# Layer 1 begun with eight units by quarters of K, and layer 0's first block cut in halves

## The chip, the cores and the metric

The kernel runs on one core of one Trainium2 chip. The metric is the device time of one execution in microseconds, the median of several runs. The engines of the core are TensorE (PE: matmuls; PEld: its weight loads), VectorE (DVE), ScalarE (ACT), GpSimd (POOL) and SyncE (SP), which issues nearly all loads here; 16 DMA engines move the data.

## The reference

A trunk of two layers on a residual stream x of 256 tokens by 2048 channels, all in float32:

```python
cond = silu(c)
for i in range(2):
    shift, scale, gate = split(cond @ ada_w[i] + ada_b[i], 3)     # ada_w[i]: 2048 x 6144
    h = rmsnorm(x, norm_w[i]) * (1 + scale) + shift
    out = ssd_mixer(h, ...) if i == 0 else mlstm_mixer(h, ...)
    x = x + gate * out
return rmsnorm(x, final_norm_w)
```

The first mixer (a state-space mixer, SSD) projects h to z (4096), x (4096), B and C (1024 each) and dt (64); x, B and C go through a causal convolution of 4 taps and a SiLU. Eight groups are mixed over the tokens, multiplied by SiLU(z), normalized per group and projected back (4096 to 2048). The second (mLSTM, 8 heads) projects h to q and k (4096 together, convolved likewise), v, o and z (4096 each) and 16 gates, mixes per head, normalizes, multiplies by SiLU(z) and projects back.

## The kernel before

**Tiles.** Channels lie on partitions, so x^T and h^T are 16 chunks (K chunks) of 128 x 256. A *unit* is a block of 512 output columns of one projection: 4 weight tiles of 128 x 2048 (a quarter of K each, 1 MB of 2^20 bytes), each loaded in two halves of 128 x 1024 into `raw` (6 buffers of 512 KB). ScalarE rounds a half to `hi`, VectorE subtracts to get `lo` (4 buffers each), and three matmuls (`hi` with the rounded h, `hi` with its rest, `lo` with the rounded h; lines 253 to 255) stand in for one of full precision. A half makes 24 matmuls of 128 x 256, a tile 48, a unit 192. Units of v keep tokens on partitions (lines 264 to 266: half as many matmuls of twice the width).

**Modulation products.** cond @ ada_w is made on VectorE: an *item* is two K chunks of 1024 columns (two loads of 512 KB), and for each chunk one operation adds `raw * cond[k]` to an accumulator `aacc` (line 77, 128 x 1024). After 8 items the accumulator is summed over partitions: 8 transposes on TensorE (line 202), each followed by an accumulating copy on ScalarE. A layer has 6 such column chunks, `cc` 0 to 3 for shift and scale of four K chunks of h each, 4 and 5 for the gate of the residual.

**Order.** The program is one list of items: weight tiles (`w`), modulation items (`a`), and steps that make chunks of h (`h`; each chunk two VectorE operations, `htmp` and `hT`, and one on ScalarE). It is written out by constants: `PRE`, `START`, `ADA_AT`, `POST`, `K1`, `DEF1`. Loads are issued on SP in the list's order, 3 items ahead; splits are issued 3 halves ahead of their matmuls. What follows a unit (convolutions, SSD, mLSTM) are Python generators that are stepped once per half (`run_bg`), so that their operations come between splits and matmuls.

**Layer 0** begins with the 9 units of `PRE`, taken by blocks of K: `START` = 4, 4, 4, 4 chunks. In each block every unit gets one weight tile. The first two units keep their two PSUM banks (pool `pj`, 4 banks) through all blocks; the other 7 use two banks of pool `pm` (4 banks, tile `ms`) for a block and are then *parked*: ScalarE copies the first block's banks to SBUF, VectorE adds those of later blocks (`park`). `ada_items(0, cc)` for the next block come between the weight tiles at the places `ADA_AT`. Then `POST` follows: further units, and three passes of the output projection (`op`), over groups 0 to 2, 3 and 4, 5 to 7. Its tuples (q, n) put n modulation items of queue q among that entry's tiles; queue 0 holds `cc` 4 and 5 of layer 0, queue 1 the chunks 0 to 3 of layer 1, but for the last `DEF1`.

**Layer 1** begins, after the row statistics (`to_layer1`: 12 chunks of h at once), with the units o and z of head 0 by quarters of K, the one late modulation item among them. Then come the gates' tile, and head by head qk, v, o and z, each unit whole. The gates' chain (`gates_done`: softplus, two scans, transposes) must be through before any head's mixing (`gen_ml`). Output passes stand after head 3 and at the end.

The lines that drive this at the beginning of layer 0 and of layer 1:

```python
cuts = grid(START)
items.extend(sh_sc(*cuts[0]))
for i, (k, n) in enumerate(cuts):
    items.append(dict(kind="h", layer=0, ks=range(k, k + n)))
```

## Time and profile before

| | |
|---|---|
| Median of 3 runs | 1799.52 us (1786.51 to 1804.31) |
| Profiled execution, first to last instruction (span) | 1784.4 us; no other time is recorded for it; the shortest run is 2.1 us above it |
| TensorE busy, mean granted clock | 1696.1 us (95%), 0.979 |
| VectorE busy | 1295.9 us (73%) |
| ScalarE busy | 923.6 us (52%) |
| Read from HBM | 390.41 MB; 220 GB/s with what is written, over the span |

Busy time is a union of the instructions' spans, and matmuls overlap, so a share of 95% is no measure of how much faster TensorE could go. The clock is the share of full speed that was granted, 0.5 or 1.0 at any moment; a stage's figure is the mean. Times in the trace are microseconds from the first instruction.

### The profile page before, as it was taken

What the parts mean: (1) busy time and instruction counts of PE and PEld (TensorE: products, weight loads), DVE (VectorE), ACT (ScalarE), POOL (GpSimd) and SP (SyncE); (2) the same over time, 40 slices, a digit from 0 to 9 for tenths busy, and PEclk for the clock granted to TensorE, in tenths of its full rate; (3) what the DMA queues carried; (4) which work ended last, traced back from release to release, by engine and by line L of the source; (5) the groups of instructions that cost most, each with busy time, mean ns of one, the idle gap of its engine ahead of it and who ended that gap; (6) DMA issues with size and microseconds to landing.
All of it is one profiled execution on the core that took longest, in us unless ns stands there. A gap on an engine that the chain in (4) does not pass through costs nothing.

```text
span 1784.4 us, 32951 instructions
## 1 busy us (share of the span) xinstructions
PE 1696.1 (95%) x13285; PEld 1633.0 (92%) x13285; DVE 1295.9 (73%) x1615; ACT 923.6 (52%) x1571; POOL 97.4 (5%) x127
## 2 busy tenths in 40 slices
PE   2999999999899899899999999999999999999997
PEld 2998999999899889899898989899989898989996
DVE  6789899999886789886777776646455555564554
ACT  3443557998553487445455445544345454454442
POOL 0000003222200020000000000000000000000000
PEclk6999999999999999999999999999999999999998
DMA  9988856566776885894666676545555555554551
GB/s 359 327 305 300 291 183 209 184 201 219 264 247 219 276 298 193 295 339 167 230 227 235 235 259 209 188 169 186 184 183 173 181 171 184 175 180 170 185 178 71
DMA packets 110377, 394.74 MB, mean 221 GB/s; under 512 B 14352, under 2 KB 14352, under 8 KB 110224
## 3 DMA queue, kind: packets, MB, share of 16 engines
q1 hardware_dynamic: 107856, 392.54, 64.5%
q8 instruction: 104, 1.70, 0.4%
q0 software_dynamic: 2368, 0.09, 0.1%
q14 instruction: 49, 0.40, 0.1%
HBM read 390.41 MB, written 2.10 MB: 220 GB/s over the span
## 4 chain that ended last, share of the span: by engine, by line
PE 68%; DVE 11%; issue 11%; DMA 5%; ACT 3%; POOL 1%; SPq 0%; ACTq 0%; POOLq 0%; DVEq 0%
PE pj L253 16%; PE pj L254 16%; PE pj L255 16%; DVE aacc L77 4%; DVE lo L81 4%; PE pj L264 3%; PE pj L265 3%; PE pj L266 3%; DMA raw<-in_ada 3%; PE ms L253 2%; PE ms L254 2%; PE ms L255 2%; ACT hi L73 1%; DMA raw<-in_wss 1%; PE ms L202 1%
## 5 line engine op out<-in xcount | busy, mean ns | idle before, releaser
L73 ACT ACTIVATE hi<-raw 128x1024 fp32r<-128x1024 f32 x548 | 580.9, 1062 | 719.9 <-PE pj L254 496.8
L81 DVE TENSOR_TENSOR lo<-raw,hi 128x1024 fp32r<-128x1024 f32 x548 | 670.0, 1225 | 321.9 <-ACT hi L73 318.9
L253 PE MATMUL pj<-hT,hi 128*128 128x256 f32 x2400 | 683.8, 285 | 4.3 <-ACT hT L73 4.3
L254 PE MATMUL pj<-hT,hi 128*128 128x256 f32 x2400 | 676.4, 282 | 0.5 <-DVE hT L77 0.5
L255 PE MATMUL pj<-hT,lo 128*128 128x256 f32 x2400 | 674.6, 281 | 1.3 <-DVE lo L81 1.3
L253 PEld LDWEIGHTS pj<-hT,hi 128*128 128x128 f32 x2400 | 456.7, 191 | 5.7 <-ACT hT L73 4.9
L254 PEld LDWEIGHTS pj<-hT,hi 128*128 128x128 f32 x2400 | 456.7, 190 | 1.7 <-issue 0.8
L255 PEld LDWEIGHTS pj<-hT,lo 128*128 128x128 f32 x2400 | 455.8, 190 | 2.1 <-DVE lo L81 1.7
L253 PE MATMUL pj<-y,hi 128*128 128x256 f32 x1024 | 292.2, 285 | 0.0
L254 PE MATMUL pj<-y,hi 128*128 128x256 f32 x1024 | 291.8, 285 | 0.0
L255 PE MATMUL pj<-y,lo 128*128 128x256 f32 x1024 | 291.4, 285 | 0.0
L77 DVE SCALAR_TENSOR_TENSOR aacc<-raw,cond,aacc 128x1024 f32<-128x1024 f32 x180 | 236.0, 1311 | 40.4 <-DMA raw<-in_ada 38.8
L253 PEld LDWEIGHTS pj<-y,hi 128*128 128x128 f32 x1024 | 197.2, 193 | 0.6 <-issue 0.3
L254 PEld LDWEIGHTS pj<-y,hi 128*128 128x128 f32 x1024 | 197.4, 193 | 0.0
L255 PEld LDWEIGHTS pj<-y,lo 128*128 128x128 f32 x1024 | 197.2, 193 | 0.0
L253 PE MATMUL ms<-hT,hi 128*128 128x256 f32 x448 | 127.2, 284 | 2.3 <-DVE park L81 2.0
L255 PE MATMUL ms<-hT,lo 128*128 128x256 f32 x448 | 126.2, 282 | 0.8 <-DVE lo L81 0.8
L254 PE MATMUL ms<-hT,hi 128*128 128x256 f32 x448 | 126.2, 282 | 0.0
L264 PE MATMUL pj<-hi,hT 128*128 128x512 f32 x256 | 101.8, 398 | 0.0
L265 PE MATMUL pj<-hi,hT 128*128 128x512 f32 x256 | 101.4, 396 | 0.0
L266 PE MATMUL pj<-lo,hT 128*128 128x512 f32 x256 | 101.2, 395 | 0.0
L253 PEld LDWEIGHTS ms<-hT,hi 128*128 128x128 f32 x448 | 85.2, 190 | 3.5 <-DVE park L81 2.6
(175 smaller groups left out, 1557.9 us busy)
## 6 DMA issues: line engine op xcount, KB each, us to landing
raw<-in_wml SPq DMA_DIRECT2D x256, 512.0 KB, 4.0
raw<-in_ada SPq DMA_DIRECT2D x192, 512.0 KB, 5.2
raw<-in_wss SPq DMA_DIRECT2D x160, 512.0 KB, 4.9
raw<-in_wso SPq DMA_DIRECT2D x64, 512.0 KB, 5.1
raw<-in_wmo SPq DMA_DIRECT2D x64, 512.0 KB, 3.6
xT<-in_xt SPq DMA_DIRECT2D x4, 512.0 KB, 6.2
out<-o SPq DMA_DIRECT2D x4, 512.0 KB, 4.0
raw<-in_wdt SPq DMA_DIRECT2D x2, 512.0 KB, 3.1
```

What stands on the lines that cost most here:

```text
L73: nc.scalar.activation(out, in_, func, **kw)
L77: nc.vector.scalar_tensor_tensor(out, a, s, b, op0, op1)
L81: nc.vector.tensor_tensor(out, a, b, op)
L202: nc.tensor.transpose(ps[:, sl], acc[:, c * P:(c + 1) * P], ident)
L253: nc.tensor.matmul(o, hi[:, w0:w0 + P], ah, start=first, stop=False, skip_group_check=True)
L254: nc.tensor.matmul(o, hi[:, w0:w0 + P], al, start=False, stop=False, skip_group_check=True)
L255: nc.tensor.matmul(o, lo[:, w0:w0 + P], ah, start=False, stop=last, skip_group_check=True)
L264: nc.tensor.matmul(o, ah[:, s], wh, start=(k == 0), stop=False)
L265: nc.tensor.matmul(o, al[:, s], wh, start=False, stop=False)
L266: nc.tensor.matmul(o, ah[:, s], wl, start=False, stop=(k == u.ktot - 1))
```

## The change

1. `START` becomes 2, 2, 4, 4, 4, and the first block's modulation comes as two parts (`ada_small`, now with 4 pieces of 256 columns per load, read by 1 KB rows): 4 items with products of 512 columns before the first two chunks of h, 4 more among the first half block's tiles, `cc` 1 among the second's. The half blocks use a half of each weight tile. Parked units are parked once more.
2. Layer 1 begins with 8 units by quarters of K (`K1`): o and z of head 0 in PSUM, qk, v of head 0 and qk, v, o, z of head 1 parked in SBUF (three of the four buffers `y`). `mm` learns to close a group of the v kind before parking.
3. `DEF1` = 16: 16 of the 32 items for shift and scale of layer 1 (`cc` 2 and 3) leave `POST` and stand one behind each tile of the first two quarters. `to_layer1` makes 8 chunks of h; the other two fours come at their quarters.
4. The gates' tile stands before the sixth tile of the fourth quarter (`GPOS` = 5). The convolution of qk waits for the gates, and from head 2 on until the scores of head h-2 are made; v, o and z of head h first complete head h-2 (`head_over`).

```diff
-ADA_AT = [[0, 2, 3, 3, 5, 5, 5, 7], [0, 0, 4, 5, 5, 5, 8, 8], [0, 0, 0, 1, 2, 3, 7, 8]]
+ADA_AT = [[0, 2, 4, 6], [0, 1, 2, 3, 4, 5, 6, 7], [0, 0, 2, 3, 4, 5, 6, 7], [0, 0, 1, 2, 3, 4, 6, 7]]
-START = [4, 4, 4, 4]
-K1, DEF1 = [("o", 0), ("z", 0)], 1
+START = [2, 2, 4, 4, 4]
+K1 = [("o", 0), ("z", 0), ("qk", 0), ("v", 0), ("qk", 1), ("v", 1), ("o", 1), ("z", 1)]
+RES1, DEF1, GPOS = 2, 16, 5
...
-POST = [('z', 4, (0, 1)), ('dt', 0, (0, 2)), ('z', 3, (0, 1)), ('x', 3, (0, 1)), ('x', 4, (0, 1)), ('z', 6, (0, 2)), ('z', 5, (0, 3)), ('bc', 3, (0, 4), (1, 1)), ('x', 6, (0, 1)), ('op', (0, 1, 2), (1, 2)), ('x', 5, (1, 3)), ('z', 7, (1, 3)), ('x', 7, (1, 6)), ('op', (3, 4), (1, 3)), ('op', (5, 6, 7), (1, 13))]
+POST = [('z', 4, (0, 1)), ('dt', 0, (0, 2)), ('z', 3, (0, 1)), ('x', 3, (0, 1)), ('x', 4, (0, 1)), ('z', 6, (0, 2)), ('z', 5, (0, 3)),
+        ('bc', 3, (0, 4)), ('x', 6, (0, 1)), ('op', (0, 1, 2), (1, 3)), ('x', 5, (1, 1)), ('z', 7, (1, 1)), ('x', 7, (1, 1)),
+        ('op', (3, 4), (1, 3)), ('op', (5, 6, 7), (1, 7))]
...
     def ada_small(layer, cc, part):
-        return [dict(kind="a", src=ada[layer, cc, 4 * part + q], hs=(0, 1), layer=layer, key=(cc, part), q=q, nq=4,
+        def half(q, j):
+            v = ada[layer, cc, 2 * q + j].rearrange("p (r c) -> p r c", r=4)
+            return v[:, :, 256 * part:256 * (part + 1)]
+        return [dict(kind="a", src=[half(q, j) for j in range(2)], hs=(0, 1), layer=layer, key=(cc, part), q=q, nq=4,
                      w=512) for q in range(4)]
...
+            if isinstance(it["src"], list):
+                nc.sync.dma_start(raw.rearrange("p (r c) -> p r c", r=4), it["src"][half])
+            else:
+                nc.sync.dma_start(raw, it["src"][:, 1024 * half:1024 * (half + 1)])
...
-                    nc.tensor.matmul(o, ah[:, s], wh, start=(k == 0), stop=False)
+                    nc.tensor.matmul(o, ah[:, s], wh, start=(fresh and kk == 0), stop=False)
                     nc.tensor.matmul(o, al[:, s], wh, start=False, stop=False)
-                    nc.tensor.matmul(o, ah[:, s], wl, start=False, stop=(k == u.ktot - 1))
+                    nc.tensor.matmul(o, ah[:, s], wl, start=False,
+                                     stop=(kk == u.nk - 1 and (closes or (u.park is not None and ends))))
...
+    qk_used = set()
+
+    def head_over(h):
+        if h >= 2:
+            finish([held[1, h - 2]])
 
     def qk_done(h):
         def f(banks):
-            qk_t[h] = sp.tile([P, 4, T], F32, tag="a4", name=nm("qk"))
-            qk_d[h] = spawn(gen_conv(banks, "mcw", "mcb", [2 * h, 2 * h + 1, 16 + 2 * h, 17 + 2 * h], qk_t[h]))
+            def conv():
+                yield from gate_ok(lambda: "gates" in held and held["gates"].over and (h < 2 or h - 2 in qk_used))
+                qk_t[h] = sp.tile([P, 4, T], F32, tag="a4", name=nm("qk"))
+                yield from gen_conv(banks, "mcw", "mcb", [2 * h, 2 * h + 1, 16 + 2 * h, 17 + 2 * h], qk_t[h])
+            qk_d[h] = spawn(conv())
             held[1, h] = spawn(gen_ml(h))
...
     st2 = OutStat()
-    first = [ml_unit(*tok, side=i >= 2) for i, tok in enumerate(K1)]
+    first = [ml_unit(*tok, park=None if i < RES1 else parker(1, i - RES1)) for i, tok in enumerate(K1)]
     for q in range(4):
         if 4 * q >= ready1:
+            assert len(late) <= DEF1 - 8 * (q + 1 - ready1 // 4)
             items.append(dict(kind="h", layer=1, ks=range(4 * q, 4 * q + 4)))
         new = w_items(first, 4 * q, 4)
         for j, w in enumerate(new):
+            if q == 3 and j == GPOS:
+                add_unit(Unit("fm", 1, 8, 1, h_act, gates_done), [wgt])
             items.append(w)
-            n = -(-len(late) // max(1, (len(new) - j) + (ready1 // 4 - 1 - q) * len(new))) if 4 * q < ready1 else 0
+            n = -(-len(late) // max(1, len(new) - j + (2 - q) * len(new))) if q < 3 else 0
             items.extend(late[:n])
             late = late[n:]
     assert not late
     m1 = len(items)
-    add_unit(Unit("fm", 1, 8, 1, h_act, gates_done), [wgt])
```

`v_done`, `o_done` and `zp_done` call `head_over(h)` first; `parker` takes the layer as a further key.

## Rows read from the trace of the kernel before

**Rows 1.** The page: span, and TensorE's busy time.

```profile
span 1784.4 us, 32951 instructions
PE 1696.1 (95%) x13285; PEld 1633.0 (92%) x13285; DVE 1295.9 (73%) x1615; ACT 923.6 (52%) x1571; POOL 97.4 (5%) x127
```

**Rows 2.** Stages: from:to, length; busy us (instructions) by engine; clock, DMA share, GB/s.

```profile
0.00:41.55 41.55, 9.30 (x43) 7.20 (x43) 27.35 (x38) 12.86 (x40) 2.88 (x9) 0.71 0.97 363
41.55:98.35 56.80, 55.07 (x440) 54.10 (x441) 46.43 (x51) 29.63 (x53) 0.00 (x0) 0.94 0.88 312
98.35:157.58 59.23, 54.81 (x442) 53.15 (x441) 51.81 (x59) 23.95 (x40) 0.00 (x0) 0.97 0.92 320
157.58:212.94 55.36, 54.03 (x443) 51.80 (x441) 48.86 (x56) 24.00 (x38) 0.00 (x0) 1.00 0.88 306
212.94:504.68 291.74, 276.92 (x2313) 268.42 (x2312) 275.21 (x359) 221.12 (x486) 61.27 (x75) 0.98 0.63 211
504.68:573.80 69.12, 69.12 (x579) 69.12 (x578) 48.10 (x59) 29.46 (x31) 0.00 (x0) 1.00 0.67 222
573.80:658.82 85.02, 80.43 (x667) 78.48 (x666) 70.54 (x76) 49.75 (x114) 7.71 (x10) 0.96 0.85 294
658.82:726.00 67.18, 61.15 (x501) 58.87 (x500) 59.88 (x84) 48.08 (x113) 4.45 (x3) 0.97 0.67 219
726.00:806.30 80.30, 73.60 (x599) 71.22 (x598) 67.77 (x77) 35.66 (x74) 0.69 (x1) 1.00 0.91 321
806.30:883.00 76.70, 73.19 (x605) 72.98 (x606) 56.84 (x86) 35.63 (x47) 1.20 (x2) 0.97 0.56 188
...
1318.76:1413.56 94.80, 94.80 (x709) 90.08 (x707) 55.02 (x69) 45.42 (x58) 1.97 (x3) 1.00 0.53 178
```

**Rows 3.** Timeline of VectorE at the start: start, us, instruction, count.

```profile
11.53 0.75 DVE L85 TENSOR_SCALAR aacc<-raw,cond 128x1024 f32<-128x1024 f32 x1 [7.03 <-DMA raw<-in_ada]
...
18.18 15.81 DVE L77 SCALAR_TENSOR_TENSOR aacc<-raw,cond,aacc 128x1024 f32<-128x1024 f32 x12
```

**Rows 4.** Timeline of TensorE: the first projection.

```profile
41.55 1.23 PE L253 MATMUL pj<-hT,hi 128*128 128x256 f32 x4 [3.31 <-ACT hT L73]
```

**Rows 5.** Waits from 574 to 659: us in total, times, longest.

```profile
DVE aacc L77 <- DMA raw<-in_ada: 11.6, 7, 3.0
...
PE ms L202 <- ACT ms L73: 3.9, 1, 3.9
```

**Rows 6.** Waits from 659 to 800: the broadcast of groups 5 to 7's norms.

```profile
PE ms L289 <- DVE dg L85: 4.9, 2, 3.4
```

**Rows 7.** Waits from 806 to 883: the gates' transposes.

```profile
PE ms L774 <- DVE gaterow L81: 3.5, 1, 3.5
```

**Rows 8.** VectorE's groups by shape: busy us, mean ns, idle before.

```profile
L81 DVE TENSOR_TENSOR lo<-raw,hi 128x1024 fp32r<-128x1024 f32 x548 | 670.0, 1225 | 321.9 <-ACT hi L73 318.9
L77 DVE SCALAR_TENSOR_TENSOR aacc<-raw,cond,aacc 128x1024 f32<-128x1024 f32 x180 | 236.0, 1311 | 40.4 <-DMA raw<-in_ada 38.8
...
L81 DVE TENSOR_TENSOR park<-park,ms 128x512 f32<-128x512 f32 x42 | 27.8, 681 | 0.6 <-PE ms L255 0.6
...
L77 DVE SCALAR_TENSOR_TENSOR hT<-htmp,mod,hT 128x256 fp32r<-128x256 f32 x32 | 13.9, 480 | 1.5 <-ACT hT L73 1.5
...
L77 DVE SCALAR_TENSOR_TENSOR zp<-th,pj 128x512 f32<-128x512 f32 x16 | 10.9, 680 | 0.0
```

**Rows 9.** The page's DMA part: packets by size; queues with packets, MB, share.

```profile
DMA packets 110377, 394.74 MB, mean 221 GB/s; under 512 B 14352, under 2 KB 14352, under 8 KB 110224
...
q1 hardware_dynamic: 107856, 392.54, 64.5%
...
q0 software_dynamic: 2368, 0.09, 0.1%
```

**Rows 10.** Timeline of VectorE: first and last operation of the gates' chain.

```profile
858.78 0.48 DVE L85 TENSOR_SCALAR gaterow<-pj,V 128x256 f32<-128x256 f32 x1 [0.44 <-PE pj L255]
...
881.56 0.42 DVE L81 TENSOR_TENSOR gaterow<-gaterow,G 128x256 f32<-128x256 f32 x1
```

More of the change, by code (lines that the diff above doesn't have):

```diff
@@ L214, in load @@
             raw = wp.tile([P, 1024], F32, tag="raw", name=nm("raw"), bufs=RAWB)
-            nc.sync.dma_start(raw, it["src"][:, 1024 * half:1024 * (half + 1)])
+            if isinstance(it["src"], list):
+                nc.sync.dma_start(raw.rearrange("p (r c) -> p r c", r=4), it["src"][half])
+            else:
+                nc.sync.dma_start(raw, it["src"][:, 1024 * half:1024 * (half + 1)])
             it["raw"][half] = raw
@@ L549, in f @@
                 i = PRE.index(("z", g)) - RES
-                sz_t[g] = atile[i // 2][:, 1024 * (i % 2):1024 * (i % 2 + 1)].rearrange("p (b t) -> p b t", b=4)
+                sz_t[g] = atile[0, i // 2][:, 1024 * (i % 2):1024 * (i % 2 + 1)].rearrange("p (b t) -> p b t", b=4)
             z_done[g] = spawn(gen_z(banks, sz_t[g]))
@@ L662, in trunk_kernel, with parker @@
     atile = {}
-    def parker(i):
+    def parker(layer, i):
         def f():
-            if i // 2 not in atile:
-                atile[i // 2] = wp.tile([P, 2048], F32, tag="y", name=nm("park"), bufs=4)
+            key = (layer, i // 2)
+            if key not in atile:
+                atile[key] = wp.tile([P, 2048], F32, tag="y", name=nm("park"), bufs=4)
             o = 1024 * (i % 2)
-            return [atile[i // 2][:, o + 512 * j:o + 512 * (j + 1)] for j in range(2)]
+            return [atile[key][:, o + 512 * j:o + 512 * (j + 1)] for j in range(2)]
         return f
-    pre = [ssd_unit(tok, side=i >= 2) for i, tok in enumerate(PRE[:RES])] + [ssd_unit(tok, parker(i)) for i, tok in enumerate(PRE[RES:])]
+    pre = [ssd_unit(tok, side=i >= 2) for i, tok in enumerate(PRE[:RES])] + [ssd_unit(tok, parker(0, i)) for i, tok in enumerate(PRE[RES:])]
     def grid(cut):
@@ L792, in f @@
         def f(banks):
+            head_over(h)
             v_t[h] = sp.tile([P, 2, 512], F32, tag="s4c", name=nm("v"))
@@ L799, in f @@
         def f(banks):
+            head_over(h)
             to_t[h] = sp.tile([P, 4, T], F32, tag="s4b", name=nm("to"))
@@ L806, in f @@
         def f(banks):
+            head_over(h)
             zp_t[h] = sp.tile([P, 4, T], F32, tag="s4a", name=nm("zp"))
@@ L829, in gen_ml @@
             nc.tensor.matmul(ps[:, T:384], k[:, c, P:T], q[:, c, P:T], start=(c == 0), stop=(c == 1))
+        qk_used.add(h)
         yield
@@ L885, in trunk_kernel, with ml_unit @@
     ML = {"qk": (0, "fm", qk_done), "v": (1, "tm", v_done), "o": (2, "fm", o_done), "z": (3, "fm", zp_done)}
-    def ml_unit(name, h, side=False):
+    def ml_unit(name, h, park=None):
         i, kind, done = ML[name]
-        return Unit(kind, 4, 2, 4, h_act, done(h), side=side), [wml[4 * h + i, q] for q in range(4)]
+        return Unit(kind, 4, 2, 4, h_act, done(h), park=park), [wml[4 * h + i, q] for q in range(4)]
     st2 = OutStat()
-    first = [ml_unit(*tok, side=i >= 2) for i, tok in enumerate(K1)]
+    first = [ml_unit(*tok, park=None if i < RES1 else parker(1, i - RES1)) for i, tok in enumerate(K1)]
     for q in range(4):
         if 4 * q >= ready1:
+            assert len(late) <= DEF1 - 8 * (q + 1 - ready1 // 4)
             items.append(dict(kind="h", layer=1, ks=range(4 * q, 4 * q + 4)))
```

## The prediction

> **What bounds the kernel now.** I read the page first, then a table of the span cut into stages, then the waits of the stages that lose time. The page gives 95% busy for TensorE over a span of 1784.4 us [rows 1], but that hides short stalls, so the stage table [rows 2] is read by three things: TensorE's idle time, its granted clock, and what VectorE and the DMA engines do meanwhile. The stage 504.68 to 573.80 is the clean one: 12 weight tiles (1.049 MB each, 48 matmuls each by the code) in 69.12 us, TensorE never idle. That is 5.76 us a tile, so a quarter of 8 units is 46.1 us and layer 0's block of 9 units 51.8 us. Against this the other stages stand thus [rows 2]:
> - The first 41.55 us hold no projection at all: VectorE starts its first products at 11.53 when their data lands and works through them until 33.99 [rows 3]; the first projection starts at 41.55 [rows 4].
> - The three blocks from 41.55 to 212.94 take 171.4 us for 155.5 us of tiles. Each loads 17 items (9 weights, 8 modulation), 17.8 MB; DMA moved 306 to 320 GB/s in them, and 3 x 17.8 MB in 171.4 us is 312. VectorE was busy 147.1 us, 86%. These blocks are fed at the rate of the loads, with VectorE close behind.
> - 212.94 to 504.68: VectorE busy 94%. The change leaves this work as it is.
> - 573.80 to 806.30 (units x5, z7, x7 and the last two output passes): 232.5 us with 17.3 us of TensorE idle (4.6, 6.0, 6.7). The clock shares of 0.96 and 0.97 cost another 3.4 and 2.0 us: 22.7 us in all. The first of its stages loads 24 items, 25.2 MB in 85 us, and there VectorE waits 11.6 us for modulation data and TensorE 3.9 us for the transposes behind them [rows 5]; the middle one waits for groups 5 to 7 [rows 6].
> - 806.30 to 883: 3.5 us of wait for the gates' chain [rows 7]. Afterwards layer 1 runs with TensorE full, VectorE at 58% and DMA at 178 GB/s (1318.76 to 1413.56) [rows 2].
>
> So layer 0 is short of loads and VectorE time, layer 1 has both to spare; each term asks which of the two the moved work meets.
>
> **Start of layer 0, block of 4 cut into 2 and 2.** The first modulation chunk is read in two parts, each 4 items whose products are 512 wide. Sixteen such products at 0.68 us (the row of a 512-wide operation with the same opcode; this and all VectorE durations below are in [rows 8]) are 10.9 us for 22.5 us, so the last is done near 22.5. Before, 7.6 us passed from the last product to the first projection; that leaves 30, and TensorE starts 11.5 us sooner. The first half block (9 half tiles, 25.9 us) covers its VectorE work: 9 splits (11.0), 4 small items (10.9) and 2 chunks of h (two 0.48 us operations each, 1.9). The second half block does not. VectorE owes 9 splits (11.0), 8 full items (16 x 1.311 less 0.56 for the cheaper first, 20.4), two chunks of h (1.9), and for the 7 parked units a further add into SBUF, 14 x 0.681 = 9.5 that did not exist before: 42.8 us against 25.9 of matmuls. Its loads are 12.5 items, 13.1 MB, 42 us at 313 GB/s. So it ends at 30 + 25.9 + 42.8, near 99 with no gaps and 105 at the 86% that VectorE reached in these blocks; before, the next block began at 98.35. From there blocks and limits are the old ones, so the difference is carried on. The modulation pieces now come in rows of 1 KB, and no packet between 512 B and 2 KB is in the trace [rows 9]. From the nearest rows: 107856 packets of 3.6 KB took 64.5% of 16 engines, 171 ns each; 2368 tiny ones took 0.1%, 12 ns each. If the 12 ns are all overhead, four 1 KB packets cost 36 ns more than one of 4 KB, 21% of the 23 us that chunk's 8.4 MB takes at 363 GB/s: 0 to 5 us. Without any gap and without that price VectorE could be through by 89: bounds -9 and +12. I take **+3**: VectorE as the limit, nearer to its 94% than to its 86%, and a little for the short rows.
>
> **Relief of late layer 0.** Fifteen of 28 modulation items leave 573.80 to 806.30 (by the order list 3, 3, 6, 3, 13 become 1, 1, 1, 3, 7). Each takes two loads off SP's queue and two products of 1.311 us off VectorE (39 us of 198), and two of the four transposed chunks go, with their 8 transposes and 8 accumulating copies each. Stage x5 to x7 then loads 15.7 MB, 53 us at its own 294 GB/s, under its 69 us of tiles: the load wait, the transposes stuck on ScalarE and the slow clock after them go, 7 of 8.0 us. The last pass loads 19.9 MB for 26.2, 62 us at 321 GB/s: 5 of 6.7 us, the rest being the row statistics. In the middle the wait is a chain of groups 5 to 7, which 22 us less VectorE work ahead shortens: 4 of 8. Together **-16**. The bounds are 6 (only what waits for loads) and 22.7 (all that is lost).
>
> **Layer 1's first quarters.** They hold 8 units instead of 2, and 16 late items stand one behind each tile of the first two. Each quarter then loads 16 items, both together 33.6 MB against 92.2 us of tiles. At the 313 GB/s of the blocks that is 107 us, +15; if the six raw buffers (3.1 MB) start full and end empty, 97 us, +5. At 294 it is 114, +22; at 363 nothing. VectorE owes 32 splits (39.2), 32 products (40.8), 12 park adds in the second quarter (8.2) and 8 chunks of h beyond the first four, which fall in the gap between layers (7.6): 95.8 us, 102 at 94% busy, 112 at 86%: +10 to +20. I take **+11** (0 to +22). The first quarter's 12 parks are copies on ScalarE and cost nothing: in the first block, with 14 of them, it was busy 29.6 of 56.8 us [rows 2]. Were it late, the four spare PSUM banks would stop the next parked unit. The last two quarters load 8 items each with 24 further adds, 16 us beside 39 of splits in 92: free.
>
> The Trainium skill (DMA: Bandwidth & Descriptors, Specifications) puts the limit of one core's HBM reads at about 358 GB/s. At that rate this stage's loads would take 94 us, its term would be that of VectorE alone (+4 with no gap, +10 at 94% busy) and the sum below -8 to -2. Only the first 41.55 us of the trace come to such a rate, so the sum goes by the blocks.
>
> **Gates and heads.** The gates' tile now stands before the last three tiles of the fourth quarter, 17 us of cover plus whatever of unit qk2 the order puts ahead; before, some 7 half tiles of qk0 stood there (605 matmuls in the stage, 432 of them o0, z0 and the gates [rows 2]). Their chain took from 858.78 to 881.98 [rows 10]. The wait was 3.5 us and slowed the clock after it (0.97 of 76.7 us): between -5 and +3, **-1**. Two heads then start together. A head's own VectorE work is 55.0 less 32 splits, 15.8 us [rows 2, 8]; two of them, the gates and the first of the other 16 modulation items meet near 985. The new waits (v, o and z of head h complete head h-2 first; the convolution of qk waits for the gates, and from head 2 on for the scores of head h-2) hold two of four PSUM banks, and behind them the next units' matmuls on TensorE. With 40% of VectorE free there I take **+2**, between 0 and +10.
>
> **Sum.** 3 - 16 + 11 - 1 + 2 = -1 us on the profiled span of 1784.4. What lies around the span I take as unchanged: the shortest timed run is 1786.5, 2.1 us above it, the median 1799.5. On the median it gives 1798. A per cent, 18 us, is about what a measurement of this kernel can tell from no change: its three runs lie 17.8 us apart.
>
> **Rivals.** (1) *The spare room of layer 1 is real* (faster): raw buffers ahead and VectorE at 100% make the quarters cost +4, late layer 0 gives back 20 and the earlier start keeps 7: -7 - 20 + 4 - 1 + 2 = -22, 1777. For it: VectorE's 94% in 212.94 to 504.68, and 363 GB/s in the first 41.55 us. Against it: no stage with 17 items a block held more than 320 GB/s.
> (2) *VectorE is the bound wherever splits, products and park adds meet* (slower): second half block and first two quarters run at 86% busy. Place: these two stretches; price: +9 and +20; with late layer 0 at -12 (chains of groups 5 to 7 not shortened), heads +4 and gates 0 this is +21, 1820. It decides from VectorE work over about 0.9 of the stage's matmul time. For it: 86% in the three blocks, and 42.8 us of work on 25.9. Against it: there the loads were as late.
> (3) *The change does not do what it says at the start*: TensorE begins 11 us sooner and the first phase ends no sooner. That is in my sum; so it moves no number further.
>
> **How the numbers follow.** The forecast, within 1%, gets 0.48: terms cancel because the same bytes and products leave one crowded stretch for another. Rival 1 gets 0.28 and rival 2 0.24, the ends of the bounds being about as far on both sides. The forecast's own range is 1782 to 1816; for 8 in 10 it reaches past both rivals' times, 1769 to 1825. Faster by over 1% 0.28, within 0.48, slower 0.24.
>
> **What would show it.** In the profile after: first projection near 30 us; the next full block near 101, TensorE idle and at half clock in the second half block; 573.80 to 806.30's work shorter by some 16 us with no wait of transposes for late products; the first two quarters of layer 1 near 103 us with VectorE over 90% and DMA over 300 GB/s, the last two near 92. Wrong would be quarters without idle TensorE (then rival 1), or a first phase that ends 8 us or more later together with quarters near 112 us (rival 2), or a stall at the first output pass of layer 1, which I price at nothing.

## The result, and the profile after

The changed kernel takes 1814.45 us (median of 5 runs, 1796.56 to 1821.28), the kernel before beside it 1790.25 us (5 runs, 1786.04 to 1804.31): a ratio of 1.0104, 95% interval 1.0056 to 1.0151. Run again on another chip (first experiment) it gave 1.0116 (1.0085 to 1.0147). So it is a good 1% slower, 10 to 27 us; the forecast was no change. The profiled execution took 1796.56 us, the shortest of the five, with a span of 1794.9 us against 1784.4: the rows below explain 10.5 us. The page of the changed kernel, answering to [rows 1]:

```profile
span 1794.9 us, 33052 instructions
PE 1696.9 (95%) x13285; PEld 1633.1 (91%) x13285; DVE 1324.7 (74%) x1684; ACT 929.8 (52%) x1583; POOL 97.2 (5%) x127
```

TensorE does the same work. VectorE has 28.8 us more; the 50 new park adds (92 operations for 42, 62.2 us for 27.8) are more than that. The stages, cut at the same events as [rows 2] (columns as there; the second and third lines are the two half blocks):

```profile
0.00:29.91 29.91, 7.90 (x39) 6.53 (x39) 17.09 (x37) 9.75 (x30) 2.40 (x9) 0.79 0.99 332
29.91:67.04 37.13, 29.87 (x221) 29.19 (x222) 31.25 (x40) 20.64 (x35) 0.00 (x0) 0.85 0.89 293
67.04:107.16 40.12, 30.07 (x234) 28.64 (x233) 35.06 (x44) 14.39 (x30) 0.00 (x0) 0.91 0.82 302
107.16:162.93 55.77, 52.91 (x434) 52.34 (x433) 51.70 (x61) 22.14 (x37) 0.00 (x0) 0.97 0.85 312
162.93:218.21 55.28, 52.71 (x443) 51.69 (x442) 52.22 (x59) 24.25 (x39) 0.00 (x0) 1.00 0.90 326
218.21:509.05 290.84, 276.01 (x2314) 267.75 (x2313) 272.04 (x355) 220.10 (x485) 61.47 (x75) 0.99 0.64 212
509.05:578.16 69.11, 69.11 (x579) 69.11 (x577) 48.53 (x59) 29.29 (x31) 0.00 (x0) 1.00 0.69 228
578.16:654.59 76.43, 76.43 (x659) 74.88 (x658) 53.82 (x60) 49.73 (x106) 6.63 (x9) 1.00 0.64 215
654.59:720.00 65.41, 61.99 (x504) 58.89 (x503) 54.02 (x77) 45.49 (x105) 4.36 (x4) 0.97 0.59 198
720.00:810.61 90.61, 75.62 (x589) 73.09 (x587) 60.25 (x70) 33.53 (x58) 0.69 (x1) 0.93 0.73 240
810.61:861.63 51.02, 49.16 (x344) 46.21 (x345) 37.84 (x46) 27.37 (x50) 0.00 (x0) 0.95 0.76 262
861.63:908.00 46.37, 45.83 (x337) 42.67 (x336) 44.95 (x54) 21.51 (x38) 0.00 (x0) 1.00 0.96 354
908.00:954.10 46.10, 46.10 (x348) 43.92 (x348) 31.06 (x36) 18.49 (x19) 0.00 (x0) 1.00 0.56 188
```

The next block's first eight matmuls, 1.0 us, run from 101.75 on, ahead of the last 36 of the second half block, which end at 107.16. Read against [rows 2]: the last full block of layer 0 begins at 218.21 for 212.94, 5.3 us later. The long middle and the clean stage are the same within 1 us. Units x5, z7 and x7 take 76.43 us for 85.02, TensorE without a gap: 8.6 us won. But the two output passes and the gap before layer 1 take 156.0 us (654.59 to 810.61) where they took 147.5: 8.5 us lost, with TensorE idle 15.0 us and the clock at 0.93 in the second of the two stretches. (The cuts at 720 here and at 726 in [rows 2] lie some 5 us inside the last pass, in both kernels alike.) So late layer 0, from which 16 us were to come, takes 232.45 us for 232.50. Layer 1 takes 401.2 us to its first output pass (810.61 to 1211.8) for 396.7.

**The start.** VectorE's and TensorE's timelines, answering to [rows 3] and [rows 4], and the one long stall of each half block:

```profile
11.85 0.49 DVE L88 TENSOR_SCALAR aacc<-raw,cond 128x512 f32<-128x512 f32 x1 [7.42 <-DMA raw<-in_ada]
...
18.24 7.05 DVE L80 SCALAR_TENSOR_TENSOR aacc<-raw,cond,aacc 128x512 f32<-128x512 f32 x9
...
29.91 0.58 PE L262 MATMUL pj<-hT,hi 128*128 128x256 f32 x1 [2.81 <-ACT hT L76]
...
50.69 0.66 PE L208 MATMUL ms<-ident,aacc 128*128 128x128 f32 x2 [7.14 <-DVE aacc L80]
...
92.02 0.66 PE L208 MATMUL ms<-ident,aacc 128*128 128x128 f32 x2 [8.60 <-DVE aacc L80]
```

TensorE begins 11.6 us sooner and gives it back in two waits, 15.7 us in all, each for the last product of a modulation chunk whose transposes stand at the head of its queue: 7.1 us in the first half block, with 120 of its 216 matmuls behind them, and 8.6 us in the second. Before, no such wait between 41 and 213 was longer than 1.1 us. The price of a 512-wide product was 0.75 us, not 0.68; VectorE's groups by shape, answering to [rows 8]:

```profile
L84 DVE TENSOR_TENSOR lo<-raw,hi 128x1024 fp32r<-128x1024 f32 x548 | 671.7, 1229 | 302.9 <-ACT hi L76 300.4
L80 DVE SCALAR_TENSOR_TENSOR aacc<-raw,cond,aacc 128x1024 f32<-128x1024 f32 x165 | 214.5, 1300 | 49.2 <-DMA raw<-in_ada 48.5
L84 DVE TENSOR_TENSOR park<-park,ms 128x512 f32<-128x512 f32 x92 | 62.2, 684 | 0.6 <-PE ms L264 0.4
L80 DVE SCALAR_TENSOR_TENSOR aacc<-raw,cond,aacc 128x512 f32<-128x512 f32 x30 | 22.5, 751 | 0.9 <-DMA raw<-in_ada 0.2
```

**Late layer 0.** The waits of the last output pass, 720 to 803 (us in total, times, longest):

```profile
ACT hi L76 <- PE pj L263: 41.9, 21, 5.3
...
DVE aacc L80 <- DMA raw<-in_ada: 14.0, 7, 4.2
...
PE ms L306 <- DVE xT L80: 8.4, 4, 2.8
```

Before, products waited 5.2 us for loads in this window and the transposes for xT once, 2.1 us. The last pass alone, from its first matmul to its last, before and after (columns as in [rows 2]):

```profile
720.60:799.44 78.84, 74.70 (x617) 73.33 (x615) 67.39 (x75) 33.88 (x60) 1.59 (x1) 1.00 0.90 313
```

```profile
715.09:802.45 87.36, 78.40 (x617) 76.51 (x615) 56.83 (x66) 34.94 (x62) 0.69 (x1) 0.96 0.73 238
```

VectorE has 10.6 us less to do and DMA moves a quarter less a second, but TensorE idles 9.0 us for 4.1 and the same matmuls take 8.5 us longer. The stretch of VectorE's timeline that shows one of the four waits, and the one before layer 1:

```profile
728.88 1.23 DVE L84 TENSOR_TENSOR lo<-raw,hi 128x1024 fp32r<-128x1024 f32 x1 [0.93 <-ACT hi L76]
734.31 1.28 DVE L80 SCALAR_TENSOR_TENSOR aacc<-raw,cond,aacc 128x1024 f32<-128x1024 f32 x1 [4.21 <-DMA raw<-in_ada]
735.51 0.87 DVE L80 SCALAR_TENSOR_TENSOR xT<-pj,mod,xT 128x256 f32<-128x256 f32 x2
...
804.86 1.28 DVE L80 SCALAR_TENSOR_TENSOR aacc<-raw,cond,aacc 128x1024 f32<-128x1024 f32 x1
806.05 0.16 DVE L318 TENSOR_REDUCE vs<-xss 128x2 f32<-128x8 f32 x1
806.17 1.28 DVE L80 SCALAR_TENSOR_TENSOR aacc<-raw,cond,aacc 128x1024 f32<-128x1024 f32 x1
807.38 0.16 DVE L88 TENSOR_SCALAR vs<-vs 128x2 f32<-128x2 f32 x1
```

From 730 VectorE stands for 4.2 us at a product whose load has not landed. The update of xT, the residual, is behind it; its matmuls end at 733.3, and TensorE's transposes for the row statistic, which read the updated xT, stand still until 736.05 (2.8 us). This comes at the end of each of the four output units. At 804.86 and 806.17 two late products stand ahead of the row statistic's own two operations, each of 0.16 us, on which layer 1's start hangs: TensorE waits 4.5 us for the broadcast of that statistic, before 0.8, and the gap between the pass and layer 1 is 8.2 us for 6.9.

In the earlier stages the waits went as forecast: products wait 4.1 us for loads between 574 and 655 and TensorE for nothing there [rows 5]; the broadcast of the group norms is waited for 3.4 us [rows 6].

**Layer 1.** The gates' stall of [rows 7] is 0.5 us instead of 3.5. The second quarter reads 354 GB/s and keeps VectorE at 44.95 of 46.37 us, and TensorE hardly idles.

### The profile page after: what moved, and what is told of

It reads as the page before. It is cut to its first block, busy times and chain, and to the rows that moved or that the text cites. A ratio compares the mean times of both kernels' runs of the same rounds, so it can differ in the third digit from the quotient of the medians.

```text
span 1794.9 us, 33052 instructions
## 1 busy us (share of the span) xinstructions
PE 1696.9 (95%) x13285; PEld 1633.1 (91%) x13285; DVE 1324.7 (74%) x1684; ACT 929.8 (52%) x1583; POOL 97.2 (5%) x127
## 4 chain that ended last, share of the span: by engine, by line
PE 63%; DVE 13%; issue 12%; DMA 6%; ACT 4%; POOL 1%; SPq 0%; ACTq 0%; DVEq 0%; POOLq 0%
PE pj L262 14%; PE pj L263 14%; PE pj L264 14%; DVE aacc L80 4%; DVE lo L84 4%; DMA raw<-in_ada 4%; PE ms L262 2%; PE ms L264 2%; PE ms L263 2%; PE pj L275 2%; PE pj L274 2%; PE pj L273 2%; DMA raw<-in_wss 2%; ACT hi L76 1%; ACT E L76 1%
## 5 line engine op out<-in xcount | busy, mean ns | idle before, releaser
L262 PE MATMUL pj<-hT,hi 128*128 128x256 f32 x2144 | 608.1, 284 | 3.9 <-ACT hT L76 3.9
L264 PE MATMUL pj<-hT,lo 128*128 128x256 f32 x2144 | 602.4, 281 | 2.9 <-DVE lo L84 2.9
L263 PE MATMUL pj<-hT,hi 128*128 128x256 f32 x2144 | 602.5, 281 | 0.1
L262 PEld LDWEIGHTS pj<-hT,hi 128*128 128x128 f32 x2144 | 406.5, 190 | 5.5 <-ACT hT L76 4.6
L264 PEld LDWEIGHTS pj<-hT,lo 128*128 128x128 f32 x2144 | 405.6, 189 | 4.4 <-DVE lo L84 3.8
L263 PEld LDWEIGHTS pj<-hT,hi 128*128 128x128 f32 x2144 | 406.5, 190 | 1.1 <-issue 0.7
L80 DVE SCALAR_TENSOR_TENSOR aacc<-raw,cond,aacc 128x1024 f32<-128x1024 f32 (+1 forms) x195 | 237.0, 1215 | 50.2 <-DMA raw<-in_ada 48.7
L262 PE MATMUL ms<-hT,hi 128*128 128x256 f32 x704 | 200.3, 285 | 2.8 <-DVE park L84 2.8
L264 PE MATMUL ms<-hT,lo 128*128 128x256 f32 x704 | 199.1, 283 | 0.0
L263 PE MATMUL ms<-hT,hi 128*128 128x256 f32 x704 | 198.8, 283 | 0.0
L262 PEld LDWEIGHTS ms<-hT,hi 128*128 128x128 f32 x704 | 134.4, 191 | 4.8 <-DVE park L84 3.0
L263 PEld LDWEIGHTS ms<-hT,hi 128*128 128x128 f32 x704 | 134.4, 191 | 0.4
L264 PEld LDWEIGHTS ms<-hT,lo 128*128 128x128 f32 x704 | 134.2, 191 | 0.0
L273 PE MATMUL pj<-hi,hT 128*128 128x512 f32 x192 | 76.6, 399 | 0.0
```

Source lines behind the costliest of these rows:

```text
L80: nc.vector.scalar_tensor_tensor(out, a, s, b, op0, op1)
L262: nc.tensor.matmul(o, hi[:, w0:w0 + P], ah, start=first, stop=False, skip_group_check=True)
L263: nc.tensor.matmul(o, hi[:, w0:w0 + P], al, start=False, stop=False, skip_group_check=True)
L264: nc.tensor.matmul(o, lo[:, w0:w0 + P], ah, start=False, stop=last, skip_group_check=True)
L273: nc.tensor.matmul(o, ah[:, s], wh, start=(fresh and kk == 0), stop=False)
```

## The experiments

All were timed in five rounds beside the kernel before; a ratio is to that kernel. "Stage" times are differences of events in the trace, as above.

**The ruler.** The kernel before against itself, and the changed kernel again.

> The kernel before against itself: how far a ratio strays from 1 without any change. If differences of 0.2% can be read, the ratio is within 0.002 of 1; if the runs of a kernel keep a level of their own, it lies further off, and the ratios from 0.998 to 1.004 of the other kernels say nothing.

> The changed kernel as it is, on the chip of the three runs beside it. In its first profile the time lies 10 us above the kernel before, in its other runs some 20 to 30 us above, at a lower granted clock. If those runs only met a slower chip, this one is 10 us above its neighbour, clock 0.98; if stalls and the clock after them vary within the kernel, 10 to 30 us again, and a profile of a later run shows more half-clock stretches than the nine of the first.

Measured: 1.0017 (1.0001 to 1.0032) and 1.0116 (1.0085 to 1.0147). The kernel before thus read 0.17% high beside itself, so 1.002 can be no change; whether 0.998 is a gain is not certain either. The later profile of the changed kernel, 6.5 us longer than the first, has nine stretches at half clock as the first had; its 6.5 us and more (517.4 for 509.0 at the first output pass) were lost ahead of that pass.

**Whole first block in the changed kernel; halves alone in the kernel before.**

```diff
-START = [2, 2, 4, 4, 4]        # and the old ADA_AT
+START = [4, 4, 4, 4]
```

> The changed kernel with the first block of layer 0 whole again (START 4, 4, 4, 4, its old ADA_AT). Theory A, that the halves cost 5 us by the park adds and short rows of the second half block and two or three extra stalls: 5 to 12 us faster than the changed kernel, block of K chunk 12 begun near 213 us instead of 218. Rival, that the start is a gain lost elsewhere: 5 or more slower than the changed kernel.

> The kernel before with the first block in halves and nothing else. If the halves are what the changed kernel pays for, the block of K chunks 12 to 15 begins 5 to 8 us later (218 to 221 instead of 212.9) and the time is 6 to 15 us longer, ratio 1.004 to 1.008. If the halves cost only together with the late relief and the quarters (the later phases reacting to the shift), the ratio is within 0.002 of 1 with the same late block.

Measured: 1.0033 (1.0016 to 1.0051) without the halves, 1.0061 (1.0041 to 1.0080) with nothing else. The two agree: the halves cost 10.4 us by the medians of the changed kernel and its whole-block variant (1806.96 less 1796.56, same chip), 11.0 by those of the halves alone. They are the larger part of the loss, and they cost as much with nothing else changed. The halves alone, first three stages:

```profile
0.00:29.70 29.70, 8.01 (x38) 6.69 (x38) 17.07 (x37) 9.75 (x30) 2.40 (x9) 0.74 0.99 333
29.70:102.13 72.43, 55.04 (x409) 53.11 (x409) 61.09 (x76) 33.98 (x64) 0.00 (x0) 0.85 0.88 303
102.13:219.39 117.26, 111.82 (x918) 109.38 (x917) 109.26 (x127) 47.42 (x77) 0.00 (x0) 0.99 0.87 312
```

The block that began at 212.94 begins at 219.39.

**Short rows or VectorE?** Four runs. In the first the kernel before reads its first modulation chunk by 1 KB rows; in the second the changed kernel reads its small parts by 4 KB rows (the data laid out for it). The third adds one VectorE operation behind each park add of one block of the kernel before (a maximum of the value with itself, 14 of them, 9.5 us); the fourth leaves out the 14 new park adds of the changed kernel.

```diff
+nc.sync.dma_start(raw.rearrange("p (r c) -> p r c", r=4), v[:, :, half, :])   # 1: rows of 1 KB
...
+return [dict(kind="a", src=ada[layer, cc, 4 * part + q], ...                 # 2: whole rows
...
+if it["ti"] == 1: vtt(dst[i], dst[i], dst[i], ALU.max)                       # 3
...
-else:
+elif not (it["ti"] == 0 and it["hs"] == (1,)):                               # 4
     vtt(dst[i], dst[i], bk, ALU.add)
```

> The kernel before, with only the first modulation chunk (8.4 MB) read by rows of 1 KB. Theory A: DMA near 300 GB/s in the first 40 us, first projection near 47 us instead of 41.5, 4 to 7 us slower than before. Rival (rows cost nothing): first projection at 41.5 to 42.5, no change.

> The changed kernel with the two parts of the first modulation chunk laid out so that each load reads rows of 4 KB again; all else as changed, half blocks and their park adds included. Theory A, that the 1 KB rows are what delays the first phase (DMA moved 332 GB/s at 99% busy in its first 30 us, against 363 at 97% before): block of K chunk 12 at 212 to 214 us instead of 218, 5 to 12 us faster than the changed kernel. Rival, that VectorE's 9.5 us of further park adds delay it: no earlier than 217, within 3 us of the changed kernel.

> The kernel before, with one more VectorE operation of 128 x 512 after each of the 14 park adds of the second block (K chunks 4 to 7), 9.5 us of VectorE time and no load. If the first phase is bound by loads (theory A): block of K chunk 12 0 to 3 us later, no change in time. If VectorE bounds it: 8 to 10 us later, the time 8 or more us longer.

> The changed kernel without the 14 park adds of the second half block: what K chunks 2 and 3 give the 7 parked units is left out. Theory A, that these adds on VectorE delay the first phase: block of K chunk 12 at 209 to 213 us instead of 218 to 221, 7 to 12 us faster than the changed kernel. Rival, that the early transposes on TensorE (7.1 and 8.6 us of wait at 50.7 and 92.0) or the loads bind: no earlier than 217.

Measured: 0.9999 (0.9975 to 1.0022), 1.0088 (1.0060 to 1.0117), 1.0054 (1.0031 to 1.0077), 1.0070 (1.0047 to 1.0093). Short rows cost a little rate and no time: the first 30 us of the first run and of the kernel before,

```profile
0.00:30.00 30.00, 6.99 (x34) 6.43 (x34) 16.60 (x24) 6.92 (x19) 2.87 (x9) 0.75 1.00 324
```

```profile
0.00:30.00 30.00, 6.37 (x34) 5.81 (x34) 17.87 (x25) 6.84 (x19) 2.88 (x9) 0.79 0.95 354
```

324 GB/s for 354, 2.2 us at the first projection, 1.4 at the last full block. Whole rows gave the changed kernel nothing back beyond the intervals (the last full block begins at 220.24 for 218.21). VectorE work does cost time there: in the third run the block with the added work takes 63.75 us for 59.23 and the next 58.77 for 55.36 [rows 2], and what follows begins at 221.02, 8.1 us later for 9.5 us of added work:

```profile
98.50:162.25 63.75, 54.68 (x443) 53.16 (x441) 57.63 (x68) 22.58 (x36) 0.00 (x0) 0.95 0.84 291
162.25:221.02 58.77, 54.41 (x443) 51.95 (x441) 50.97 (x60) 25.22 (x41) 0.00 (x0) 1.00 0.84 294
```

Leaving out the half block's adds brings the last full block back to 215.3, so they explain about half of the delay. The half blocks themselves end hardly sooner without them: the next block begins at 105.4, where the second half block ended at 107.16 with eight of the next block's matmuls inside it. The other half of the delay is not taken apart: ScalarE waits 20.4 us for loads in the second half block, and a TensorE queue with the transposes behind the block's matmuls was not run.

**Raw buffers.** The changed kernel with 7 buffers instead of 6 (room from two small tiles), and with 5.

```diff
-RAWB, HIB, E6B = 6, 4, 2
+RAWB, HIB, E6B = 7, 4, 2       # cbm and t1: 2 buffers for 3;   second run: 5, 4, 2 alone
```

> The changed kernel with 7 raw buffers for loads instead of 6 (the room taken from two small tiles, 3 to 2 buffers each). Theory: in the last output passes loads are not late for want of bandwidth but because SP issues each one only when a split has freed a raw buffer, so a product stands at the head of VectorE's queue until its load lands. Then one buffer more lets each load go out about 2.5 us earlier: the waits of products for loads fall from 14 us between 720 and 803 to under 7, those of the transposes for xT from 8.4 us to about 4, and the time is 5 to 10 us shorter than the changed kernel's, ratio 1.004 to 1.008. Rival: the waits come from the order of the instructions alone, they stay within 3 us, ratio 1.009 to 1.012.

> The changed kernel with 5 raw buffers instead of 6, nothing else. If raw buffers pace the loads, the waits of products for loads in the last output pass grow from 14 us to over 20 and the fed phases (the first 218 us, the second quarter of layer 1) get longer too: 15 us or more, ratio 1.02 or more. If the order of the instructions sets the waits, the ratio stays at 1.009 to 1.012.

Measured: 1.0066 (1.0041 to 1.0092) and 1.0182 (1.0152 to 1.0212). With seven buffers time and waits go the theory's way, the waits less far than it said; with five they do not go the other way. There the first phase is what grows (the last full block begins at 232.56, 14 us later), and the last pass is not worse: the waits there of the 7-buffer and then of the 5-buffer kernel, over the same 83 us before the pass ends,

```profile
DVE aacc L80 <- DMA raw<-in_ada: 9.6, 6, 2.9
...
PE ms L306 <- DVE xT L80: 4.8, 3, 1.8
```

```profile
DVE aacc L80 <- DMA raw<-in_ada: 10.8, 7, 3.0
...
PE ms L306 <- DVE xT L80: 4.0, 3, 1.9
```

Both are below the 14.0 and 8.4 us of six (11.8 to 14.0 and 6.9 to 8.4 us in four profiles with six). So too few buffers is not what makes products wait in the last pass; their place in the queue relative to the load is what is left, and the next runs change it. Why five and seven both wait less is not shown.

**Other places for the products.** Late layer 0 of the changed kernel with no item in the last pass (they go to the passes and units before); with its whole first block and the last pass's 7 items put behind middle tiles of the output units, the 16 of layer 1 spread into the third quarter; and with a whole first block, 10 items in the first pass and none in the last.

```diff
-('op', (0, 1, 2), (1, 3)), ('x', 5, (1, 1)), ('z', 7, (1, 1)), ('x', 7, (1, 1)), ('op', (3, 4), (1, 3)), ('op', (5, 6, 7), (1, 7))
+('op', (0, 1, 2), (1, 4)), ('x', 5, (1, 2)), ('z', 7, (1, 2)), ('x', 7, (1, 2)), ('op', (3, 4), (1, 6)), ('op', (5, 6, 7))    # 1
...
+        if i % 3 == 1: out.extend(mine[:2])                                                                                   # 2
...
+('op', (0, 1, 2), (1, 10)), ('x', 5, (1, 1)), ('z', 7, (1, 1)), ('x', 7, (1, 1)), ('op', (3, 4), (1, 3)), ('op', (5, 6, 7))   # 3
```

> The changed kernel with the 7 modulation items of layer 0's last output pass moved ahead of it (op 0 to 2: 4, x5, z7, x7: 2 each, op 3 and 4: 6, last pass none). Theory A, that products waiting for their loads stand on VectorE in front of the residual updates, so that TensorE waits at the end of each of the four output units: the four waits (2.8, 2.0, 2.1, 1.6 us) and the slow clock after them go, 8 to 12 us faster than the changed kernel. Rival, that TensorE waits there for VectorE or ScalarE whatever stands ahead: within 3 us of it.

> The changed kernel with the first block whole, the 7 items of the last output pass placed behind the middle tile of each unit (2, 2, 2, 1) instead of evenly, and the 16 late items spread from the third tile of layer 1's first quarter into its third. Theory A: no wait of TensorE for residual updates behind a product that waits for its load, gap between layers 1 to 2 us shorter, first two quarters at 92 to 94 us: 5 to 12 us faster than the whole-first-block run (ratio about 0.998 of before). Rival, that the products only move the waits (loads 2 at a time come as late): same as that run, 1.003.

> Whole first block, quarters with 16 late items, 10 items in the first output pass, 1 each in x5, z7, x7, 3 in the second pass and none in the last. Theory A: no wait for residual updates behind products in the last pass, so the last two passes 139 to 141 us instead of 144.5 and 3 to 7 us faster than the whole-first-block run (1.000). Rival: another wait comes in their place, 1.003.

Measured: 1.0094 (1.0068 to 1.0120), 1.0039 (1.0014 to 1.0064), 1.0020 (1.0000 to 1.0040). In the last pass the products' places are what counts. With the same 7 items behind middle tiles, and with none (the second run and the third; columns as in [rows 2]), it takes

```profile
711.39:792.26 80.87, 76.51 (x616) 74.81 (x614) 54.15 (x63) 35.29 (x62) 1.59 (x1) 0.98 0.70 245
```

```profile
720.09:794.85 74.76, 73.42 (x608) 72.35 (x606) 42.53 (x48) 33.16 (x46) 0.69 (x1) 1.00 0.54 187
```

for 87.36 us (85.6 with a whole first block alone), and 75.8 in the first run. With none, TensorE waits for xT inside the pass only 0.4 to 0.6 us; 3.7 to 3.9 us are left at its end, where the first items of layer 1 stand ahead of the last update. But each time another stage pays. In the first, the broadcast of the group norms waits behind the products instead, up to 5.3 us at a time (660 to 825):

```profile
PE ms L299 <- DVE dg L88: 9.8, 4, 5.3
...
PE ms L306 <- DVE xT L80: 4.5, 2, 3.9
```

In the second, layer 1's quarters pay (407.8 us to the first output pass). In the third, the first output pass does (76.4 us for 69.1): it loses there what the last two passes and the gap win (144.7 us, against 152.6 with a whole first block alone).

**Relief inside layer 0.** The kernel before, its items of x5 to x7 moved into the first output pass; and spread evenly.

```diff
-('op', (0, 1, 2), (1, 2)), ('x', 5, (1, 3)), ('z', 7, (1, 3)), ('x', 7, (1, 6)), ('op', (3, 4), (1, 3)), ('op', (5, 6, 7), (1, 13))
+('op', (0, 1, 2), (1, 10)), ('x', 5, (1, 1)), ('z', 7, (1, 1)), ('x', 7, (1, 2)), ('op', (3, 4), (1, 3)), ('op', (5, 6, 7), (1, 13))   # 1
...
+('op', (0, 1, 2), (1, 6)), ('x', 5, (1, 2)), ('z', 7, (1, 2)), ('x', 7, (1, 2)), ('op', (3, 4), (1, 5)), ('op', (5, 6, 7), (1, 13))    # 2
```

> The kernel before, with 8 products moved within layer 0: the first output pass, where TensorE never idles, takes 10 items instead of 2, x5, z7 and x7 take 1, 1 and 2 instead of 3, 3 and 6. Nothing goes to layer 1. If the crowding of x5 to x7 is worth 8 us by itself (theory A): that stage 76 to 78 us instead of 85, the first pass 69 to 71, 5 to 9 us faster than before (ratio 0.995 to 0.997). Rival, that the gain comes back in the last two passes whatever was moved (as in the changed kernel, where they took 3 to 7 us longer): no change.

> The kernel before with the 31 items of queue 1 placed evenly: 6 in the first output pass (2 before), 2 in each of x5, z7 and x7 (3, 3, 6 before), 5 in the second pass (3), 13 in the last. If x5 to x7 lose 8 us to their loads alone and the passes have room for a few items more, that stage takes 77 us for 85 and the first pass stays at 69 to 71: 5 to 8 us gained, ratio 0.996. If every stage of late layer 0 is as full of VectorE work as any other, the waits move and the ratio is within 0.002 of 1.

Measured: 0.9980 (0.9959 to 1.0001) and 0.9983 (0.9967 to 0.9998); beside the latter, on the same chip, the kernel before read 1.0017 (1.0001 to 1.0032). The even spread is thus faster than the changed kernel, and than the kernel before by 2 us (1786.47 to 1788.48 of the runs beside it) to 5 us (1791.55 when run again). Its stages (first pass, x5 to x7, the rest):

```profile
511.70:581.70 70.00, 69.57 (x580) 69.37 (x579) 54.74 (x66) 29.52 (x32) 0.00 (x0) 1.00 0.77 269
581.70:661.10 79.40, 77.97 (x665) 75.60 (x665) 58.24 (x68) 51.90 (x122) 6.73 (x10) 1.00 0.74 251
661.10:809.84 148.74, 135.92 (x1098) 130.09 (x1096) 131.52 (x161) 81.23 (x176) 5.60 (x5) 0.98 0.80 282
```

Ten items in the first pass are too many: it takes 78.70 us for 69.12, with one stall of 4.9 us of TensorE behind `xs`. Six cost 0.9 us, and x5 to x7 still give 5.6.

**The quarters.** Eight units by quarters with a whole first block and one late item (2 and 4 of the change); with 8 late items; and the first of these with ten items in the first output pass, as in the run above.

```diff
-RES1, DEF1, GPOS = 2, 16, 5
+RES1, DEF1, GPOS = 2, 1, 5      # 1 and 3;  2: DEF1 = 8, one behind every second tile
```

> Only the 8 units by quarters (with the gates moved and the new waits of heads); start, POST and the late item as in the kernel before. Theory A: the quarters cost little without the moved products, 0 to +4 us against the kernel before, the first two quarters 92 to 95 us. Rival, that parking and two heads at once are themselves the cost: +8 or more, with waits for park adds or heads after the fourth quarter.

> Whole first block, quarters, but only 8 items late, behind every second tile of layer 1's first quarters, and layer 0's other 24 with 9 in the first output pass, 1 each in x5, z7, x7, then 3 and 8. Theory A: x5 to x7 76 us, first two quarters near 94 us, ratio to before 0.994 to 0.999. Rival, that products in the quarters cost what they save: 1.001 to 1.004, as with 16.

> Whole first block, eight units by quarters with one late item, and the items of x5 to x7 moved into the first output pass: the parts of the change that cost nothing, with the relief put where the other run had it. If the gains of quarters (gates' wait, 3.5 us) and of the moved items (3.6 us) add, the ratio is 0.995 to 0.997. If the runs' spread is all there is, 0.998 to 1.002.

Measured: 1.0015 (0.9996 to 1.0033), 1.0090 (1.0062 to 1.0118), 1.0001 (0.9978 to 1.0024). The quarters alone cost and gain nothing: 395.8 us to layer 1's first output pass for 396.7. Eight late items are no cheaper than sixteen. That kernel puts 9 items into the first output pass, which takes 77.60 us with the same 4.9 us stall, and from the start of layer 1 to its first output pass it needs 408.9 us; its second quarter alone takes 56.4 us, in which products wait 20.2 us for loads and TensorE idles 6.7 us. In the last run no gain shows; whether those of quarters and first pass would add, the intervals do not tell.

## Why the prediction was wrong

Single profiles of one kernel differ by several us in a stage, so the terms are means over profiled executions that share the edit. For START these are eleven with the whole first block and six with halves; for the other terms five of each (the kernel before, again, with quarters alone, with short rows, with halves alone; the changed kernel, again, with whole block, with whole rows, with 7 buffers), for layer 1 without the quarters four:

| term | predicted | measured | from |
|---|---|---|---|
| START, to the beginning of the first output pass | +3 | +9.0 | 508.1 to 517.1 |
| of it to the last full block | | +6.5 | 212.9 to 219.4 |
| late layer 0 | -16 | -4.9 | 234.5 to 229.6 |
| of it x5 to x7 | -7 | -8.9 | 85.3 to 76.4 |
| of it the second output pass | -4 | -2.9 | 62.9 to 60.0 |
| of it the last pass and the gap | -5 | +6.9 | 86.3 to 93.2 |
| layer 1 to its first output pass | +12 | +6.1 | 396.2 to 402.3 |
| its first output pass | 0 | +1.6 | 69.2 to 70.8, with quarters alone too |
| sum | -1 | +11.8 | |

**The step that failed is the relief of late layer 0, -16**, and in it "5 of 6.7 us" in the last pass. It took the loss there for a shortage of loads and VectorE time, which fewer items would cure. Where that was so, in x5 to x7, the gain came in full, and in the second pass most of it. In the last pass it was not: VectorE is busy 57 of 87 us and DMA at 238 GB/s, and TensorE idles more than before. What stops it there is a short chain in the wrong place: a product at the head of VectorE's queue whose load has not landed, xT's update behind it, transposes behind that. With 7 items for 13 the remaining products waited longer (14.0 us for 5.2). That the products there do it, by their place more than by their amount, is shown by the runs: the pass takes 78.8 us with 13 items, 87.4 with 7, 80.9 with the same 7 elsewhere, 74.8 and 75.8 with none; that other stages then pay, by their times. Why a load is late at 238 GB/s is only argued: SP waits for splits to free raw buffers, and the splits wait for TensorE through ScalarE's `hi` (41.9 us there, 26.8 before), but 5 and 7 buffers both had shorter waits than 6.

**START, +3**, failed too, in the step "The first half block (9 half tiles, 25.9 us) covers its VectorE work". The first projection came as forecast (29.91 for 30), but that half block took 37.1 us: the transposes of the second part stand in TensorE's queue ahead of more than half of its matmuls and wait there for VectorE's products, and the mean clock was 0.85. The second took some 39 us for 42.8 to 49.8, since VectorE had begun on its products at 55.0. It also makes four chunks of h (for the next block), not two, 1.9 us more. Over both VectorE was busy 66.3 of 77.3 us: the 86% of the blocks before, which the prediction used for the second half block's upper value alone. That the next block's first matmul came at 101.75 for a forecast of 101 is luck: it ran ahead of 36 matmuls of the half block. "From there blocks and limits are the old ones" held (55.8 and 55.3 us for 59.2 and 55.4). The +9.0 agrees with the 10 to 11 us by the time of the runs; what it has beyond the +6.5 lies in the long middle, which varies from 291 to 302 us among these profiles (the first output pass begins between 504 and 513 us with the whole block, 509 and 523 with halves). Short rows alone cost nothing, and six raw buffers are just enough for the first phase (five cost 14 us there, seven gain nothing). That VectorE's work sets the length of a full block is shown by the added operations (9.5 us cost 8.1); of the delay by halves the new adds explain about half.

**Layer 1's quarters, +11**: too dear. The first two take 97.4 us for 92.2. The prediction's "no stage with 17 items a block held more than 320 GB/s" was no limit of the loads: here they held 354. The Trainium skill (DMA: Bandwidth & Descriptors, Specifications) puts the limit of one core's reads at about 358 GB/s. The trace shows more: 354 in that quarter, but 382 from 3 to 43 us in the kernel before, so the figure of the Trainium skill does not bound this kernel. VectorE was busy 82.8 us in these quarters, not 95.8; which of the rest was done before and after them was not counted; in the second it ran at 97% without stopping TensorE. What price there is, is that of the late items: the quarters alone cost nothing.

**Gates and heads**: the stall shrank by 3 us, and from 908 on no wait of TensorE is longer than 1.4 us: the +2 for the heads did not come. That layer 1's first output pass takes 1.6 us more with quarters was priced at nothing and is not explained.

**The rivals.** Rival 1 is wrong: the spare room of layer 1 was real (the quarters cost 5 us, near its 4), but late layer 0 did not give back 20 and the start did not keep 7. Rival 2 has the sign and, by the ratios (18.6 and 20.8 us), nearly its price of 21, but half its reasons: its +9 for the start holds, its quarters (+20) do not, and late layer 0 gave back 5 where it had 12; that the number came so near is partly luck.

The sum by stages, +11.8, lies within the first measurement's interval (10 to 27 us) and below the second's (15 to 26). Both profiled executions of the changed kernel are the shortest of their runs, that of the kernel before run again is the third longest of its twelve; what the longer executions lose was not profiled.

## What to carry to other kernels

Before counting a stage's idle time as shortage, look at which engine is full in it: where none is, the stall is a chain with an in-order queue in it, and removing work from the stage can lengthen it. An operation whose data come late must not stand in a queue just ahead of one that the bottleneck waits for. Starting the bottleneck earlier gains nothing when the engine that feeds it is nearly full up to the next meeting point; and before moving work to another phase, spread it evenly within the one it is in, which here won 2 to 5 us with one line.

## What the runs showed of the hardware

**A pause on GpSimd behind a broadcast.** The operation `rs` (two numbers a partition, 0.73 us) starts only some 10 us after the PARTITION_BROADCAST ahead of it ended, with nothing shown that it waits for; in the changed kernel:

```profile
469.81 1.49 POOL L579 PARTITION_BROADCAST acb<-acb  x1 [4.16 <-DMA acb<-acs]
481.16 0.73 POOL L290 TENSOR_TENSOR rs<-vs,nhalf 128x2 f32<-128x2 f32 x1 [9.86 <-issue]
```

In the kernel before it was 7.84 us, in the run without the half block's adds 12.04. Between these profiles it varies by 4 us, as much as some effects sought here, and the broadcast that uses `rs` comes behind it. The profile's spans on GpSimd are rough, so the PARTITION_BROADCAST may itself last longer than shown; no run tells the two apart.

**A product of half the width costs 58% of a whole one**, 751 to 1300 ns (the groups by shape above): cutting an operation in two has its price.
